# Raw-x products with two shift columns at three norms, and two-by-two wide tiles, in a two-layer encoder trunk

## The chip, the cores and the metric

The kernel runs on one core of one Trainium2 chip. The metric is the device time of one execution in microseconds (us); less is better. The engines are TensorE (PE in the profile; its weight loads are PEld), VectorE (DVE), ScalarE (ACT), GpSimd (POOL) and SyncE (SP), which issues the loads.

## The reference, cut

Sequence 256, model width D = 2048, two layers, all float32. Each sub-layer's norm is modulated by a shift, a scale and a gate that come from the conditioning vector c through a large matrix (adaLN: 12288 outputs a layer).

```
for l in range(2):
    sh_a, sc_a, g_a, sh_m, sc_m, g_m = split(silu(c) @ w_ada[l] + b_ada[l], 6)
    h = rmsnorm(x) * (1 + sc_a) + sh_a
    proj = h @ w_in[l]                 # differential q, k, v; latents cq, ckv; rope key
    out_a = diff_attention(...)        # 4 heads of two maps
    out_b = mla_attention(rmsnorm(cq, g) @ w_uq, rmsnorm(ckv, g) @ w_ukv, ...)
    x = x + g_a * (concat(out_a, out_b) @ w_o[l])
    h = rmsnorm(x) * (1 + sc_m) + sh_m
    x = x + g_m * (square(relu(h @ w_mlp_in[l])) @ w_mlp_out[l])   # 2048 -> 8192 -> 2048
return rmsnorm(x) * final_norm_g
```

Here rmsnorm(x) = x / rms, with rms the root of the mean square over the 2048 features of a token.

## The kernel before

**Layout.** x stays on the chip, features on partitions: 16 row blocks of 128 features by 256 tokens (`self.x[:, k]`). A product h @ w is made as output tiles of 128 features by 256 tokens, summed in PSUM over 16 row blocks k. There are eight PSUM banks of 512 columns (`bank`).

**Precision.** Trunk products run in the reduced-precision format fp32r with each factor split in a high and a low part. `mac` (L177 to L179) issues three matmuls for a step: hi·hi, hi·lo and lo·hi. In the names of the profile, `ps<-h,hi` at L177 is h's high part with the weight's, L178 h's low part, L179 the weight's low part.

**Weights.** `weights` brings a tile of 128x2048 (or 128x1536) floats through SP's queue into one of five shared buffers (`raw`), ScalarE writes its two halves' `hi` (L141), VectorE the `lo` (L142). Four `hi` and four `lo` buffers hold two tiles, so conversion runs at most two tiles ahead. The same five buffers take the adaLN tiles (`ada`, 1 MB each, 192 in all); VectorE multiplies and sums each with the conditioning vector (L292). `rate` (the RATE constants) says how many adaLN tiles are loaded for each weight tile; `ada_need` (L317) forces, in the order of the plan, all those that a use needs and that are not there yet.

**Three ways to make tiles.** `by_k` (L214) takes a weight tile by rows: for a row block, all its output tiles, in up to eight banks. It is used behind a norm, where row blocks of h become ready one by one. `pair` (L204) makes two output tiles in one bank with `mac`. `wide` (L188) makes one tile from a 512-column matmul (the weight's high part with h's high and low parts side by side, L197) and a 256-column one (its low part, L198), alternating; two banks' halves are then added (`joined`, L788). Layer 0's MLP uses `pair`, layer 1's `wide`.

**A norm.** Squares of x are summed on VectorE (`sumsq`). `rstd` (L475) sums over partitions with one-column matmuls (L483), takes root and reciprocal of two columns, builds a diagonal matrix (L492) and multiplies ones by it (L493), so that 1/rms stands on every partition for each token. `modulated` makes h for two row blocks (L503 to L505), and `norm_then_by_k` (L529) goes on with `by_k` over the first 12 output tiles: half of `w_a` or `w_m0`.

**A layer.** Norm, input projection, attention, output projection: four row groups in by_k form (`w_oa`) for tiles 0 to 3, then `pair` for the twelve others (`w_ob`), each followed by `update` (x plus gate times product, L786) and `sumsq`. Then the second norm with `w_m0`, and `mlp`: four blocks of 16 hidden tiles (`w_m1`, then `relu2`), each multiplied with its part of the second matrix token by token in 512 columns (`rows`, L753, tiles `py`), summed in `y`, and turned back (`turned`, L762, tiles `yt`). Layer 1 starts with a norm and `w_a` again.

**What sets the order.** A scheduler orders each engine's instructions by the program and by when it expects operands. Only inside `mlp` TensorE keeps the order of the program.

## Time and profile before

| | us |
|---|---|
| median of 3 runs | 2257.03 (2255.21 to 2258.25) |
| profiled execution | 2257.35 |
| its span in the profile | 2255.3 |
| TensorE busy | 2187.8 |
| VectorE busy | 1578.3 |
| ScalarE busy | 1112.4 |
| GpSimd busy | 1.9 |

The span runs from the first to the last instruction recorded; 2.05 us lie around it. Busy times are sums of records, in which matmuls that are pipelined overlap their neighbours, so how long a matmul occupies TensorE is read from the distance of two starts, or from a stage's length divided by its matmuls. In rows of groups the last part tells how long the engine had idled ahead of them, and what ended it; in rows of the timeline the same stands in brackets.

### The profile page before, as it was taken

What the parts mean: (1) busy time and instruction counts of PE and PEld (TensorE: products, weight loads), DVE (VectorE), ACT (ScalarE), POOL (GpSimd) and SP (SyncE); (2) the same over time, 40 slices, a digit from 0 to 9 for tenths busy, and PEclk for the clock granted to TensorE, in tenths of its full rate; (3) what the DMA queues carried; (4) which work ended last, traced back from release to release, by engine and by line L of the source; (5) the groups of instructions that cost most, each with busy time, mean ns of one, the idle gap of its engine ahead of it and who ended that gap; (6) DMA issues with size and microseconds to landing.
All of it is one profiled execution on the core that took longest, in us unless ns stands there. A gap on an engine that the chain in (4) does not pass through costs nothing.

```text
span 2255.3 us, 33208 instructions
## 1 busy us (share of the span) xinstructions
PE 2187.8 (97%) x13516; PEld 1972.3 (87%) x13516; DVE 1578.3 (70%) x2047; ACT 1112.4 (49%) x1608; POOL 1.9 (0%) x10
## 2 busy tenths in 40 slices
PE   3999999999999999999999999999999999999997
PEld 2899889998899899899879998999888888888886
DVE  7889878887777777777788776666545545555555
ACT  2655654355454355345444465544645534544543
POOL 0000000000000000000000000000000000000000
PEclk9999999999999999999989999999999999999998
DMA  9988678898888878888769756665555555555551
GB/s 371 355 313 318 256 277 318 307 339 324 317 317 299 326 296 313 329 302 307 292 235 346 277 225 224 243 229 167 205 198 190 188 188 188 187 195 196 187 187 56
DMA packets 85258, 585.52 MB, mean 260 GB/s; under 512 B 9457, under 2 KB 9841, under 8 KB 20593
## 3 DMA queue, kind: packets, MB, share of 16 engines
q1 hardware_dynamic: 85106, 583.42, 70.1%
q8 instruction: 105, 1.72, 0.3%
q14 instruction: 47, 0.39, 0.0%
HBM read 581.28 MB, written 2.10 MB: 259 GB/s over the span
## 4 chain that ended last, share of the span: by engine, by line
PE 92%; DVE 5%; DMA 1%; ACT 1%; issue 1%; SPq 0%; DVEq 0%; ACTq 0%
PE py L753 31%; PE ps L197 9%; PE ps L177 7%; PE ps L178 7%; PE ps L179 7%; PE pk L177 5%; PE pk L178 4%; PE pk L179 4%; PE ps L198 4%; DVE ada L292 2%; PE pk L234 1%; PE pv L250 1%; PE pv L248 1%; PE pv L249 1%; PE po L880 1%
## 5 line engine op out<-in xcount | busy, mean ns | idle before, releaser
L142 DVE TENSOR_TENSOR lo<-raw,hi 128x1024 fp32r<-128x1024 f32 (+1 forms) x728 | 861.2, 1186 | 587.4 <-ACT hi L141 586.1
L141 ACT ACTIVATE hi<-raw 128x1024 fp32r<-128x1024 f32 (+1 forms) x728 | 747.1, 1029 | 895.4 <-PE py L753 380.3
L753 PE MATMUL py<-hi,hid 128*128 128x512 f32 x2048 | 560.5, 390 | 0.0
L753 PEld LDWEIGHTS py<-hi,hid 128*128 128x128 f32 x2048 | 383.9, 188 | 79.4
L292 DVE SCALAR_TENSOR_TENSOR ada<-ada,cond 128x2048 f32<-128x2048 f32 x192 | 438.3, 2286 | 7.3 <-ACT cond L336 6.8
L753 PE MATMUL py<-lo,hid 128*128 128x512 f32 x1024 | 326.0, 389 | 0.0
L197 PE MATMUL ps<-h,hi 128*128 128x512 f32 x832 | 294.1, 399 | 0.0
L177 PE MATMUL ps<-h,hi 128*128 128x256 f32 x1024 | 291.4, 285 | 0.0
L179 PE MATMUL ps<-h,lo 128*128 128x256 f32 x1024 | 291.2, 284 | 0.0
L178 PE MATMUL ps<-h,hi 128*128 128x256 f32 x1024 | 290.8, 284 | 0.0
L198 PE MATMUL ps<-h,lo 128*128 128x256 f32 x832 | 234.0, 281 | 0.0
L753 PEld LDWEIGHTS py<-lo,hid 128*128 128x128 f32 x1024 | 192.3, 188 | 39.8
L177 PE MATMUL pk<-h,hi 128*128 128x256 f32 x752 | 214.5, 290 | 3.9 <-ACT h L504 3.9
L178 PE MATMUL pk<-h,hi 128*128 128x256 f32 x752 | 215.4, 287 | 1.1 <-DVE h L505 1.1
L179 PE MATMUL pk<-h,lo 128*128 128x256 f32 x752 | 215.0, 287 | 0.0
L177 PEld LDWEIGHTS ps<-h,hi 128*128 128x128 f32 x1024 | 196.5, 192 | 0.4
L178 PEld LDWEIGHTS ps<-h,hi 128*128 128x128 f32 x1024 | 196.6, 192 | 0.4
L179 PEld LDWEIGHTS ps<-h,lo 128*128 128x128 f32 x1024 | 196.6, 192 | 0.3
L197 PEld LDWEIGHTS ps<-h,hi 128*128 128x128 f32 x832 | 156.4, 188 | 38.8
L198 PEld LDWEIGHTS ps<-h,lo 128*128 128x128 f32 x832 | 157.4, 189 | 0.1
L177 PEld LDWEIGHTS pk<-h,hi 128*128 128x128 f32 x752 | 146.6, 198 | 6.2 <-ACT h L504 6.2
L178 PEld LDWEIGHTS pk<-h,hi 128*128 128x128 f32 x752 | 147.3, 196 | 1.5 <-DVE h L505 1.5
(209 smaller groups left out, 2568.6 us busy)
## 6 DMA issues: line engine op xcount, KB each, us to landing
raw<-in_w_m SPq DMA_DIRECT2D x232, 1024.0 KB, 4.9
ada<-in_w_ada SPq DMA_DIRECT2D x192, 1024.0 KB, 5.0
raw<-in_w_ob SPq DMA_DIRECT2D x24, 1024.0 KB, 5.0
raw<-in_w_m SPq DMA_DIRECT2D x32, 768.0 KB, 4.4
raw<-in_w_dv SPq DMA_DIRECT2D x16, 1024.0 KB, 4.8
raw<-in_w_a SPq DMA_DIRECT2D x20, 768.0 KB, 6.6
raw<-in_w_t SPq DMA_DIRECT2D x12, 1024.0 KB, 5.6
w<-in_w_a SPq DMA_DIRECT2D x24, 384.0 KB, 5.5
```

The source lines that it names most:

```text
L141: nc.scalar.activation(hi, v, AF.Copy)
L142: ins = nc.vector.tensor_tensor(lo, v, hi.bitcast(F32), ALU.subtract)
L177: mm(ps, hi, x[0], start=first, stop=False, skip_group_check=shared)
L178: mm(ps, hi, x[1], start=False, stop=False, skip_group_check=shared)
L179: mm(ps, lo, x[0], start=False, stop=last, skip_group_check=shared)
L197: mm(ps.rearrange("p a b -> p (a b)"), hi, both, start=k == 0, stop=False)
L198: mm(ps[:, 0], lo, x, start=False, stop=k == nk - 1)
L234: self.nc.tensor.matmul(ps, w[i][:, j * P : j * P + P], whole[i], start=first, stop=last, skip_group_check=True)
L248: mm(ps, xh, hi, start=first and k == 0, stop=False)
L249: mm(ps, xh, lo, start=False, stop=False)
L292: ins = nc.vector.scalar_tensor_tensor(w, w, 1.0, self.cond, ALU.mult, ALU.mult, accum_out=acc[:, i : i + 1])
L753: nc.tensor.matmul(out, stationary, v, start=start, stop=stop)
```

## The change

It does four things.

1. At three norms (layer 0's MLP, layer 1's attention, layer 1's MLP) the first six output tiles are multiplied with x·(1+scale) instead of h, as soon as a row block of x is complete (`ahead_part`). Two columns more hold the shift, twice the same, made by two small GpSimd operations for two row blocks, so a matmul has 258 columns. The six banks (`pa`) are multiplied with 1/rms and given the shift's product when they leave PSUM (`scaled`, `relu2` with a bias). `ahead_rest` puts the norm's sum over partitions behind step 1 of 8; from step 2 on, `modulated` makes h for everything else. The six other tiles of the by_k stage join the tiles behind it.
2. `rstd` sums with a matrix of 1/n, so that root and reciprocal work on 256 columns on all partitions; the diagonal is gone.
3. `wides` takes two tiles together, all 512-column matmuls of both ahead of all 256-column ones. It replaces `pair` in layer 0's MLP, `wide` in layer 1's, and by_k and `pair` for layer 1's differential q and k (`two`).
4. TensorE keeps the program's order from the `ob` pairs on, no more from the MLP on alone.

```diff
+TX = T + 2
+NAHEAD = 6
...
-    def wide(self, src, xs):
-
-        ps = self.bank("ps")
+    def wides(self, srcs, xs):
+
+        mm = self.nc.tensor.matmul
         nk = len(xs)
-        w = self.weights(src, nk * P)
         per = nk // 2
-        mm = self.nc.tensor.matmul
-        for k, (x, _, both) in enumerate(xs):
-            hi, lo = (v[:, (k % per) * P : (k % per) * P + P] for v in w[k // per])
-            mm(ps.rearrange("p a b -> p (a b)"), hi, both, start=k == 0, stop=False)
-            mm(ps[:, 0], lo, x, start=False, stop=k == nk - 1)
-        return ps
-
-    def wides(self, srcs, xs):
-        return [self.wide(src, xs) for src in srcs]
+        pss = [self.bank("ps") for _ in srcs]
+        ws = [self.weights(src, nk * P) for src in srcs]
+        part = lambda w, i, k: w[k // per][i][:, (k % per) * P : (k % per) * P + P]
+        for ps, w in zip(pss, ws):
+            for k, (_, _, both) in enumerate(xs):
+                mm(ps.rearrange("p a b -> p (a b)"), part(w, 0, k), both, start=k == 0, stop=False)
+        for ps, w in zip(pss, ws):
+            for k, (x, _, _) in enumerate(xs):
+                mm(ps[:, 0], part(w, 1, k), x, start=False, stop=k == nk - 1)
+        return pss
...
     def rstd(self, acc, n):
 
         nc = self.nc
-        ps = [self.bank("pn") for _ in range(2)]
-        r = self.s("rms")
+        ps = self.bank("pn")[:, 0]
         acc = acc[:2] + acc[3:]
         for i, a in enumerate(acc):
-            for t in range(2):
-                nc.tensor.matmul(
-                    ps[t][:, 0, :1], a[:, t * P : (t + 1) * P], self.ones[:, :1], start=i == 0, stop=i == len(acc) - 1
-                )
-        for t in range(2):
-            nc.scalar.activation(r[:, t : t + 1], ps[t][:, 0, :1], AF.Sqrt, bias=self.eps, scale=1.0 / n)
+            nc.tensor.matmul(ps, self.mean[n], a, start=i == 0, stop=i == len(acc) - 1)
+        r = self.cp.tile([P, T], F32, tag="rstd", name=self.name("rstd"), bufs=2)
+        nc.scalar.activation(r, ps, AF.Sqrt, bias=self.eps)
         nc.vector.reciprocal(r, r)
-        d = self.tp.tile([P, T], F32, tag="t", name=self.name("diag"))
-        for t in range(2):
-            c = slice(t * P, (t + 1) * P)
-            nc.vector.tensor_scalar(d[:, c], self.ident, r[:, t : t + 1], None, ALU.mult)
-        nc.tensor.matmul(ps[0][:, 1], self.ones, d, start=True, stop=True)
-        return ps[0][:, 1]
-
-    def modulated(self, r, k, sh, sc, whole):
+        return r
+
+    def ahead(self, l, sh, sc, src):
+
+        return SimpleNamespace(l=l, sh=sh, sc=sc, src=src, parts=[], banks=None, r=None)
+
+    def ahead_part(self, st, k):
+
+        nc = self.nc
+        for g in (st.sh, st.sc):
+            self.ada_need(st.l, g, k + 1)
+        sh, sc = self.mod[st.l, st.sh], self.mod[st.l, st.sc]
+        hi, lo = (self.flat(s, F32R).rearrange("p (a b) -> p a b", a=2) for s in ("ah", "al"))
+        both = sh[:, k : k + 2].unsqueeze(2).broadcast_to([P, 2, 2])
+        nc.gpsimd.tensor_copy(hi[:, :, T:], both)
+        nc.gpsimd.tensor_tensor(lo[:, :, T:], both, hi[:, :, T:].bitcast(F32), ALU.subtract)
+        for i in range(2):
+            x, c = self.x[:, k + i], sc[:, k + i : k + i + 1]
+            nc.scalar.activation(hi[:, i, :T], x, AF.Copy, scale=c)
+            nc.vector.scalar_tensor_tensor(lo[:, i, :T], x, c, hi[:, i, :T].bitcast(F32), ALU.mult, ALU.subtract)
+            st.parts.append((hi[:, i], lo[:, i]))
+
+    def ahead_step(self, st, p):
+
+        if st.banks is None:
+            st.banks = [self.bank("pa").rearrange("p a b -> p (a b)") for _ in range(NAHEAD)]
+        for i, w in enumerate(self.weights(st.src[p], 2 * NAHEAD * P)):
+            k = 2 * p + i
+            for j, ps in enumerate(st.banks):
+                self.mac(ps[:, :TX], w, j * P, P, st.parts[k], k == 0, k == NK - 1)
+
+    def ahead_rest(self, st, first, acc, after):
+
+        h = []
+        for p in range(first, 8):
+            if p == after:
+                r = self.rstd(acc, D)
+            self.ahead_step(st, p)
+            if p >= after:
+                upto = NK * (p - after + 1) // (8 - after)
+                while len(h) < upto:
+                    h += self.modulated(r, len(h), self.mod[st.l, st.sh], self.mod[st.l, st.sc])
+        st.r = r
+        return h
+
+    def scaled(self, st, b, out):
+
+        nc = self.nc
+        c = self.s("ac")
+        for i in range(2):
+            ps = st.banks[b + i]
+            nc.scalar.activation(c[:, i : i + 1], ps[:, T : T + 1], AF.Copy)
+            nc.vector.tensor_tensor(out[:, i], ps[:, :T], st.r, ALU.mult)
+        return out, c
+
+    def modulated(self, r, k, sh, sc, whole=None):
...
+            def two(i, dst, scale):
+                ps = self.wides([io["w_q"][0, i + j] for j in range(2)], h)
+                dst.append(self.joined(ps, self.u("qk"), scale))
+
+            two(0, q, qs)
+            two(8, kk, -1.0)
+            ckv += self.latent([ckr], gkv)
+            for hd in range(1, HD):
+                two(2 * hd, q, qs)
+                probs(hd - 1)()
+                two(8 + 2 * hd, kk, -1.0)
+                if hd == 1:
+                    cq += self.latent(cqr, gq)
+            keys()
...
-        for m in range(0, NK, 2):
-            if m < 4:
-                self.update(m, banks[m // 2], g)
-            else:
+        st = self.ahead(l, 3, 4, io["w_m0"][l])
+        for m in range(0, 4, 2):
+            self.update(m, banks[m // 2], g)
+            acc = self.sumsq(acc, self.x[:, m : m + 2])
+            self.ahead_part(st, m)
+        with self.tc.manual_schedule(engines={mybir.EngineType.PE}):
+            for m in range(4, NK, 2):
                 self.update(m, self.pair([io["w_ob"][l, m - 4 + j] for j in range(2)], o), g)
-            acc = self.sumsq(acc, self.x[:, m : m + 2], m == NK - 2)
-
-        self.rate = RATE_K
-        h, banks = self.norm_then_by_k(l, acc, 3, 4, io["w_m0"], 3, 0)
-        self.rate = RATE_M
-        g = self.mod[l, 5]
-        with self.tc.manual_schedule(engines={mybir.EngineType.PE}):
-            return self.mlp(l, h, banks, g)
-
...
+        nxt = None if l == DEPTH - 1 else self.ahead(l + 1, 0, 1, io["w_a1"][0])
         for fb in range(NFB):
             hid = []
-            for m in range(0 if fb else 12, NK, 2):
-                srcs = [io["w_m1"][l, NK * fb + m + j - 12] for j in range(2)]
-                ps = self.wides(srcs, h) if l else self.pair(srcs, h)
-                for b in banks:
-                    hid += self.relu2(b)
-                banks = []
-                hid += self.relu2(self.joined(ps, self.t("sum")) if l else ps)
+            for m in range(0 if fb else NAHEAD, NK, 2):
+                pss = self.wides([io["w_m1"][l, NK * fb + m + j - NAHEAD] for j in range(2)], h)
+                if m == NAHEAD and fb == 0:
+                    for b in range(0, NAHEAD, 2):
+                        hid += self.relu2(*self.scaled(st, b, self.t("sum")))
+                hid += self.relu2(self.joined(pss, self.t("sum")))
...
+                if cols == (3,) and nxt:
+                    self.ahead_step(nxt, 0)
...
+        acc = self.turned(3, y, g, acc, nxt, nxt is None)
+        if nxt:
+            self.rate = RATE_K
+            return self.ahead_rest(nxt, 1, acc, 2), nxt
+        return acc, None
...
         for m in range(4 * c, 4 * c + 4, 2):
...
             self.update(m, ps, g)
             acc = self.sumsq(acc, self.x[:, m : m + 2], last and m == NK - 2)
+            if nxt:
+                self.ahead_part(nxt, m)
```

In the diff's last hunks, the first two lines with `nxt` stand in the loop over `py` of layer 0's last block (`mlp`), the last ones in `turned`. Not shown: the weights are laid out anew (`w_m0` and `w_a1` hold six tiles, `w_q` layer 1's q and k, `w_m1` the rest), `joined` takes a scale, `stream` is written out in `rows`, the conditioning vector is scaled by 2048 against the 1/2048 in the new matrix.

**How instructions move.** The first place is SP's queue of loads at the end of layer 0's output projection (`raw<-in_w_ob` and `raw<-in_w_m` are weight tiles, `ada` adaLN tiles). Before:

```order
L153 DMA raw_3723<-in_w_ob 128x2048
L284 DMA ada_3735<-in_w_ada 128x2048
L153 DMA raw_3785<-in_w_ob 128x2048
L284 DMA ada_3796<-in_w_ada 128x2048
L153 DMA raw_3852<-in_w_ob 128x2048
L284 DMA ada_3864<-in_w_ada 128x2048
L153 DMA raw_3914<-in_w_ob 128x2048
L284 DMA ada_3925<-in_w_ada 128x2048
L153 DMA raw_4014<-in_w_m 128x1536
```

And now:

```order
L158 DMA raw_3824<-in_w_ob 128x2048
L289 DMA ada_3835<-in_w_ada 128x2048
L289 DMA ada_3892<-in_w_ada 128x2048
L289 DMA ada_3895<-in_w_ada 128x2048
L158 DMA raw_3908<-in_w_ob 128x2048
L289 DMA ada_3918<-in_w_ada 128x2048
L158 DMA raw_3968<-in_w_ob 128x2048
L289 DMA ada_3979<-in_w_ada 128x2048
L289 DMA ada_4036<-in_w_ada 128x2048
L289 DMA ada_4039<-in_w_ada 128x2048
L158 DMA raw_4057<-in_w_m 128x1536
```

The loads alternated one to one; now one or three adaLN tiles stand between two weight tiles. From the first `ob` tile to the first `w_m0` tile there are 21 adaLN loads, 13 before; in the eight `w_m0` tiles there are five.

The second place is VectorE's queue at the same point: the last `ob` tile's low halves (`lo`, 128x1024), the update of x from the last bank, and the first `w_m0` halves (128x768). Before:

```order
L142 TENSOR_TENSOR lo_3917<-raw_3914,hi_3916 128x1024
L142 TENSOR_TENSOR lo_3921<-raw_3914,hi_3920 128x1024
L292 SCALAR_TENSOR_TENSOR ada_3864,macc_82<-ada_3864,cond 128x2048
L142 TENSOR_TENSOR lo_4017<-raw_4014,hi_4016 128x768
L142 TENSOR_TENSOR lo_4021<-raw_4014,hi_4020 128x768
L786 SCALAR_TENSOR_TENSOR x<-ps_3851,mod_77,x 128x256 x2
```

And now (`al` is the low part of x·(1+scale), `acc` the sum of squares):

```order
L147 TENSOR_TENSOR lo_3975<-raw_3968,hi_3974 128x1024
L297 SCALAR_TENSOR_TENSOR ada_3918,macc_80<-ada_3918,cond 128x2048
L297 SCALAR_TENSOR_TENSOR ada_3979,macc_80<-ada_3979,cond 128x2048
L297 SCALAR_TENSOR_TENSOR ada_4036,macc_82<-ada_4036,cond 128x2048
L858 SCALAR_TENSOR_TENSOR x<-ps_3907,mod_77,x 128x256 x2
L313 TENSOR_TENSOR mod_79<-macc_80,vec 128x2
L297 SCALAR_TENSOR_TENSOR ada_4039,macc_82<-ada_4039,cond 128x2048
L478 TENSOR_TENSOR acc_3171<-acc_3171,sqx_4031 128x512
L311 SCALAR_TENSOR_TENSOR mod_81<-macc_82,vec 128x2
L147 TENSOR_TENSOR lo_4060<-raw_4057,hi_4059 128x768
L510 SCALAR_TENSOR_TENSOR al_4044<-x,mod_81,ah_4043 128x256 x2
L147 TENSOR_TENSOR lo_4064<-raw_4057,hi_4063 128x768
```

Between the last `ob` half and the first `w_m0` half stood one adaLN sum; now four stand there, with the last update of x and the accumulation.

The third place is TensorE at layer 0's MLP norm, from the last `ob` matmul on. Before:

```order
L179 MATMUL ps_3851<-do_3062,lo_3921 128x256
L483 MATMUL pn_3981<-ones,sqa_3977 128x1
L483 MATMUL pn_3982<-ones,sqa_3977 128x1
L483 MATMUL pn_3981<-ones,sqa_3979 128x1
L483 MATMUL pn_3982<-ones,sqa_3979 128x1
L493 MATMUL pn_3981<-diag_3995,ones 128x256
L177 MATMUL pk_3999<-h_4006,hi_4016 128x256
L177 MATMUL pk_4000<-h_4006,hi_4016 128x256
L177 MATMUL pk_4001<-h_4006,hi_4016 128x256
```

And now, at the start of the `pa` matmuls and, in the second fence, behind step 1, 72 of them later:

```order
L184 MATMUL ps_3907<-do_3037,lo_3975 128x256
L182 MATMUL pa_4051<-ah_3173,hi_4059 128x258
L183 MATMUL pa_4051<-al_3174,hi_4059 128x258
L184 MATMUL pa_4051<-ah_3173,lo_4060 128x258
L182 MATMUL pa_4052<-ah_3173,hi_4059 128x258
```

```order
L183 MATMUL pa_4056<-al_3187,hi_4111 128x258
L184 MATMUL pa_4056<-ah_3186,lo_4112 128x258
L487 MATMUL pn_4152<-acc_3171,mean_100 128x256 x2
L182 MATMUL pa_4051<-ah_3325,hi_4160 128x258
L183 MATMUL pa_4051<-al_3326,hi_4160 128x258
L184 MATMUL pa_4051<-ah_3325,lo_4161 128x258
```

The sum over partitions (`pn`) stood between the last product of the old stage and the first of the new; now it stands inside the new one, and the first `pa` matmuls need the `lo` half of the first `w_m0` tile.

165 lines of the change are left out of this document (93 added, 72 removed).

## The prediction

> **What bounds the kernel now.** I read the busy shares first, then the chain that ended last.
>
> ```profile
> PE 2187.8 (97%) x13516; PEld 1972.3 (87%) x13516; DVE 1578.3 (70%) x2047; ACT 1112.4 (49%) x1608; POOL 1.9 (0%) x10
> PE 92%; DVE 5%; DMA 1%; ACT 1%; issue 1%; SPq 0%; DVEq 0%; ACTq 0%
> ```
>
> TensorE sets the time. The span goes down only where it streams less or waits less, and up where something is late for it. Next the stages, as windows (columns: stretch, its length, busy time of PE, PEld, DVE, ACT, POOL, granted clock, DMA share, GB/s). In order they are: the start; layer 0's `ob` tiles; the gap of its MLP norm (A); that MLP's by_k stage; its `py` and pair stages; the gap ahead of layer 1 (B) and the by_k stage behind it; the gap of layer 1's MLP norm (C) and its by_k stage; layer 1's `wide` stage.
>
> ```profile
> 125.00:157.00 32.00, 30.43 (x244) 29.53 (x243) 29.84 (x38) 12.60 (x17) 0.00 (x0) 1.00 0.99 380
> 357.70:427.60 69.90, 69.90 (x586) 69.90 (x585) 62.79 (x74) 27.25 (x30) 0.00 (x0) 1.00 0.91 349
> 427.60:433.50 5.90, 2.19 (x14) 1.53 (x13) 5.39 (x12) 3.03 (x7) 0.00 (x0) 0.93 0.93 319
> 433.50:505.30 71.80, 71.52 (x575) 71.52 (x576) 62.29 (x85) 36.59 (x55) 0.00 (x0) 0.96 0.87 314
> 528.30:615.40 87.10, 87.10 (x388) 72.17 (x387) 62.96 (x61) 38.38 (x41) 0.00 (x0) 1.00 0.84 317
> 615.40:707.50 92.10, 92.10 (x768) 92.06 (x767) 68.09 (x74) 47.69 (x63) 0.00 (x0) 1.00 0.84 311
> 1156.00:1167.10 11.10, 6.20 (x27) 4.88 (x26) 7.70 (x16) 2.96 (x7) 0.00 (x0) 0.67 0.60 211
> 1167.10:1262.00 94.90, 94.68 (x767) 94.68 (x768) 77.12 (x100) 45.16 (x62) 0.00 (x0) 0.97 0.83 299
> 1515.40:1521.20 5.80, 3.41 (x22) 2.55 (x20) 3.25 (x9) 2.23 (x6) 0.00 (x0) 0.74 0.40 135
> 1521.20:1592.00 70.80, 70.52 (x575) 70.53 (x576) 42.05 (x64) 36.44 (x55) 0.00 (x0) 0.97 0.53 176
> 1701.70:1792.10 90.40, 90.40 (x513) 78.49 (x512) 48.96 (x62) 51.81 (x78) 0.00 (x0) 1.00 0.54 188
> ```
>
> Two things stand here. Layer 0 runs with VectorE at 90% in the `ob` stage and the DMA at 91%, where 99% was 380 GB/s: little is free there. Layer 1's MLP has room in both.
>
> **Streaming.** The pair stage is 768 matmuls of 256 columns in 92.1 us: 119.9 ns each. The `py` stage is 384 of 512 columns (four records are its neighbours') in 87.1 us: 226.8 ns. The `wide` stage is 256 pairs of one 512 and one 256 in 90.4 us: 353.1 ns a pair, more than 119.9 + 226.8 = 346.7. The new `wides` runs all 512 first, then all 256, so a k step of a tile pair's half costs 346.7 where three by three cost 359.7: 13.0 ns saved against pairs, 6.4 against the alternating form. An output pair has 32 such steps. Layer 0's MLP has 29 pairs (12.1 us), layer 1's q and k eight (3.3), its MLP 26 alternating ones (5.3) and three that were by_k (1.2): 21.9 us. The 864 matmuls of 258 columns: 256 and 512 lie 106.9 ns apart for 256 columns, so two columns are 0.8 ns, 0.7 us together (ends 0 and, if 258 were priced as 512, 92; it is nearest to 256). **−21.2 us.**
>
> The saving rests on 13 ns that every matmul costs beside its columns (119.9 − 106.9). The Trainium skill ("TensorE: Matmul & The Clock Gate", section Back-to-back issue gap) gives columns / 2.4 + 2.5 ns for matmuls without weight loads. By that fixed part the saving would be some 4 us (an estimate from the page). The two rows above, with a weight load for each matmul, disagree with it.
>
> **The three waits that go.** Gap A is 5.9 us, and its by_k stage 71.8 for 576 matmuls that stream in 69.1: 8.6 in all. B is 11.1 plus 94.9 − 92.1 (768 matmuls): 13.9. C is 5.8 plus 70.8 − 69.1: 7.5. Together 30.0. The work of TensorE that stays is the sum over partitions and B's transposes.
>
> ```profile
> 73.39 10.52 PE L234 MATMUL pk<-hf,w 128*128 128x256 f32 x48
> 1156.23 0.33 PE L769 MATMUL yt<-ident,y 128*128 128x128 f32 x1
> 1156.91 0.98 PE L769 MATMUL yt<-ident,y 128*128 128x128 f32 x7 [0.35 <-DVE y L729]
> ```
>
> A full-precision pass of 256 columns takes 219 ns here; the new `pn` is two matmuls of two passes, 0.9 us, three times. With B's eight transposes, 1.7 us from 1156.23 to 1157.89, 4.4 us stay. **−25.6 us.** The new chain from x to 1/rms (update, square, accumulation, `pn`) is hidden by the `pa` matmuls of steps 0 and 1, 8.7 us long (72 × 0.121), if those are fed; root and reciprocal lie beside step 2.
>
> **The wait that comes: A.** `ahead_part` needs shift and scale of each row block while the `ob` tiles still run. So adaLN loads that were spread by the rate are forced earlier: 21 of them now stand between the first `ob` tile and the first `w_m0` tile on SP's queue, 13 before, and their sums stand ahead of the weight halves in VectorE's queue.
>
> ```profile
> L142 DVE TENSOR_TENSOR lo<-raw,hi 128x1024 fp32r<-128x1024 f32 x624 | 762.1, 1224 | 539.6 <-ACT hi L141 538.7
> L142 DVE TENSOR_TENSOR lo<-raw,hi 128x768 fp32r<-128x768 f32 x104 | 99.1, 957 | 47.8 <-ACT hi L141 47.4
> L292 DVE SCALAR_TENSOR_TENSOR ada<-ada,cond 128x2048 f32<-128x2048 f32 x192 | 438.3, 2286 | 7.3 <-ACT cond L336 6.8 <-DMA ada<-in_w_ada 0.5
> L505 DVE SCALAR_TENSOR_TENSOR h<-ht,mod,h 128x256 fp32r<-128x256 f32 x64 | 28.5, 481 | 0.0
> L472 DVE TENSOR_TENSOR acc<-acc,sqx 128x512 f32<-128x512 f32 x33 | 22.7, 688 | 1.0 <-ACT sqx L471 0.4
> 351.34 1.22 DVE L142 TENSOR_TENSOR lo<-raw,hi 128x1024 fp32r<-128x1024 f32 x1
> 420.64 2.36 DVE L142 TENSOR_TENSOR lo<-raw,hi 128x1024 fp32r<-128x1024 f32 x2
> 428.11 0.88 DVE L786 SCALAR_TENSOR_TENSOR x<-ps,mod,x 128x256 f32<-128x256 f32 x2 [1.16 <-PE ps L179]
> ```
>
> Queued back to back, instructions overlap by some 85 ns (the two halves take 2.36, not 2 × 1.22), so I take 1.14, 0.87, 2.21, 0.395 and 0.605 us for these five. From the first `ob` half to the first `w_m0` half VectorE has 24 halves (27.4), 21 sums (46.4), ten small sums of modulation (0.8), 16 updates of x (6.3), seven accumulations (4.2), 14 new low parts (5.5) and the first 768 half (0.9): 91.5 us, and I add two waits of 1.16 for a finished bank, 93.8. TensorE streams those twelve tiles in 12 × 48 × 0.1199 = 69.1. VectorE starts 6.6 us ahead (351.34 against the stage at 357.9). So TensorE comes out 93.8 − 6.6 − 69.1 = 18.1 us late. The DMA agrees: 33 tiles of 1.049 MB are 34.6 MB, 91 us at 380 GB/s, on the edge; I add 1.2 us for that. In the `pa` stage VectorE has 16 halves, five sums and 32 steps of the modulation, 37 us with its rests, against TensorE's 34.8 (288 × 0.121), which leaves a tail I take as 1.9. **+21.2 us**; the ends are 0 (the scheduler's queue is not in the way) and 31 (the DMA at 349 GB/s, below).
>
> **B and C.** Ahead of layer 1 the adaLN loads aren't denser (rate K), but VectorE has 16 halves (13.9), five sums (11.1) and 32 modulation steps (12.6) and some 4.4 us of the last row blocks, 42 us against 34.8. The two tiles converted ahead in the `py` stage cover about five; **+2.2** (ends 0 and 7.2). At C no adaLN load is left and DVE is at 59% of the old stage: 0. The adaLN loads that were moved up at A are missing later, in layer 0's MLP, whose DVE had 24 us to spare in 92: it only gets lighter, worth nothing.
>
> **Small edits.** Nine norms lose the diagonal step, two records each, and with it a trip from VectorE to TensorE:
>
> ```profile
> L493 PE MATMUL pn<-diag,ones x18: 377/416/767, 29.1 to 2245.6; 128*128 128x256 f32 x18
> 420.56 0.16 DVE L308 TENSOR_TENSOR mod<-macc,vec 128x2 f32<-128x2 f32 x1
> L839 DVE RECIPROCAL r<-tot 128x2 f32<-128x2 f32 x32 | 5.2, 161 | 4.3 <-ACT sm L836 2.2 <-ACT s L836 2.0
> L793 DVE TENSOR_TENSOR sum<-ps,sum 128x256 f32<-128x256 f32 x52 | 21.7, 418 | 0.3 <-ACT sum L792 0.3
> ```
>
> In each of the four latent norms two passes of 0.22 go, −1.8 in all; at the end these and the trip, an estimate of −1. The RECIPROCAL grows from two to 256 columns. At two it costs 161 ns, as the TENSOR_TENSOR of two columns does, so I take that operation's 0.42 for 256; the ends are 0.16 and, since two columns hide a dearer one, 2 us. At A, B, C step 2 hides it; in the four latents and at the end it stands on the path, 0 to +8 us. Scaling on leaving PSUM (three times six matmul results, 0.42 each) and joining layer 0's and q's halves lie on VectorE beside 11.1 us of streaming a pair, of which it uses about nine (four halves 4.6, 1.3 sums 3.0, joining and splitting 1.3); that is the thinnest cover, worth +1 by my guess at lost waits (0 to 5).
>
> **Sum**, against the profiled execution: 2257.35 (span 2255.3 and 2.05 around it, 0.3 above the median 2257.03): −21.2 −25.6 +21.2 +2.2 −2.8 +1 = −25.2, so **2232 us**.
>
> **The rivals.**
>
> *VectorE's queue is not in the way at A* (the scheduler puts halves ahead of sums, or its lead is larger). For it: before, VectorE was 6.6 us ahead with 90% of the stage filled. Against: 91.5 us of work. Then 21.2 and 2.2 go: 2208. Chance 0.12.
>
> *The DMA, not VectorE, sets A.* 34.6 MB at the 349 GB/s of the old `ob` stage are 99 us, 8 more, and with the tail 2 more: 2242. Against it: that stage's DMA was not asked for more. 0.15.
>
> *Slower: the fast rows do not hold for 512-column streams into two banks in turn.* Other 512-column matmuls of the program show a longer record than `py`:
>
> ```profile
> L753 PE MATMUL py<-hi,hid 128*128 128x512 f32 x2048 | 560.5, 390 | 0.0
> L248 PE MATMUL pv<-hi,h 128*128 128x512 f32 x128 | 53.0, 414 | 0.0
> ```
>
> If `wides` ran like `pv`, 24 ns more on its 2112 wide matmuls are +51: 2283. It turns into a loss from 25.2 / 2112 = 12 ns on. Against it: the alternating form lies only 6.4 ns above the sum of its parts. 0.06.
>
> *GpSimd blocks VectorE.* The change puts 48 small operations there, 16 at each norm. The only price in the trace is a memset.
>
> ```profile
> L812 POOL MEMSET kr<- 128x512 f32 x2 | 1.1, 526 | 1143.2 <-PE yt L769 1032.3 <-PE pb L427 111.0
> ```
>
> If each held VectorE for that long at A, where its queue is the path, 16 × 0.526 = 8.4 us: 2240. No run before shows the two engines side by side. The Trainium skill ("SBUF — State Buffer", section Who interferes with whom) says that a VectorE operation with two SBUF inputs, which `lo` and `ada` are, and a GpSimd one that reads SBUF exclude each other for a whole instruction. 0.06.
>
> *The streaming saves nothing* (the fixed 13 ns belong to the weight load and stay with the columns): 2232 + 21 = 2253, within 0.2%. The rows speak against it. 0.03.
>
> **How the numbers follow.** The forecast has 0.58. Its own terms, one up and one down, give 2222 to 2241. The range goes down to the first rival and up past the second and the GpSimd case: 2208 to 2246; outside lie the two last dear cases and the edge, about 0.1 to 0.2. A measurement of this kernel tells some 0.2%, 4.5 us, from no change: faster is the forecast, the first, second and GpSimd cases but for their tails, 0.89; same 0.05; slower 0.06.
>
> **What would show it.** In the changed profile layer 0's `ob` stage lasts 88 us, not 69.9, with VectorE near full and TensorE waiting for `lo`; the three gaps shrink to a `pn` of 0.9 us inside `pa`; layer 0's MLP stages of four pairs take 88.8 us, not 92.1, and layer 1's 88.8, not 90.4. I am wrong if the `ob` stage keeps 70 us, if those stages keep 92.1, or if TensorE waits behind `scaled` or the 256-column reciprocal.

## The result, and the profile after

The changed kernel takes 2275.45 us (median of 4 runs, 2272.99 to 2276.42) against 2256.12 for the kernel before (4 runs): a ratio of 1.0083, with a 95% interval of 1.0065 to 1.0100. It is slower by some 19 us. The forecast was 2232, with a range up to 2246. One execution of a_half_load below took 2443.96 us at a granted clock of 0.84, and is left out of the figures of that kernel.

The first lines of the profile of the changed kernel (its profiled execution took 2272.99 us) are the busy times and the chain that ended last:

```profile
PE 2178.0 (96%) x12154; PEld 1889.0 (83%) x12154; DVE 1627.9 (72%) x2166; ACT 1159.2 (51%) x1731; POOL 38.5 (2%) x59
PE 89%; DVE 7%; DMA 1%; ACT 1%; issue 1%; DVEq 0%; ACTq 0%; SPq 0%
```

TensorE issues 1362 records fewer and is busy 10 us less, and VectorE's share of the chain went from 5% to 7%. So the change did its streaming work, and put waits in somewhere. The same stages as in the prediction, as windows of the changed kernel: layer 0's `ob` tiles; steps 0 and 1 of its `pa` stage; the other six steps; `py`; wide tiles; the `pa` stage ahead of layer 1 with the last transposes; the `pa` stage of layer 1's MLP; its wide tiles.

```profile
362.40:453.70 91.30, 74.60 (x580) 73.17 (x578) 86.33 (x109) 32.14 (x44) 9.70 (x9) 0.92 0.97 365
453.70:466.40 12.70, 10.87 (x71) 10.61 (x72) 9.98 (x14) 4.92 (x8) 1.58 (x2) 0.74 0.80 285
466.40:499.40 33.00, 27.53 (x222) 26.80 (x221) 31.06 (x53) 18.64 (x34) 0.00 (x0) 1.00 0.68 250
556.60:645.60 89.00, 89.00 (x387) 72.18 (x386) 65.31 (x66) 37.72 (x41) 0.00 (x0) 1.00 0.86 324
645.60:735.20 89.60, 89.60 (x512) 78.27 (x511) 67.95 (x85) 53.26 (x79) 0.00 (x0) 1.00 0.79 300
1184.30:1226.30 42.00, 39.30 (x300) 37.98 (x299) 40.11 (x66) 23.36 (x39) 0.00 (x0) 0.96 0.71 249
1534.00:1569.40 35.40, 35.40 (x294) 35.30 (x294) 31.02 (x54) 22.98 (x40) 0.00 (x0) 1.00 0.55 194
1714.50:1804.10 89.60, 89.60 (x513) 78.24 (x513) 46.05 (x60) 53.68 (x79) 0.00 (x0) 1.00 0.50 183
```

Three things are to be seen. The `ob` stage takes 91.3 us where its matmuls stream in 69.1, with VectorE at 95% and the DMA at 97%; the two `pa` windows take 45.7 instead of 34.8 + 0.9. At layer 1's MLP norm nothing waits: 35.4. And the `py` window, whose 384 matmuls the change did not touch, takes 89.0 us where it took 87.1, with TensorE busy all through at full clock: 231.8 ns a matmul, not 226.8.

From the starts of the stages' first matmuls in the two traces (us) comes where the time went; the forecast column splits the sum of the prediction over the same stretches (without its +1 for lost waits and the 0.7 for 258 columns).

| stretch | before | after | difference | forecast |
|---|---|---|---|---|
| start to layer 0's `ob` tiles | 357.7 | 362.4 | +4.7 | −0.9 |
| `ob` tiles to the first `py` (A) | 170.6 | 194.2 | +23.6 | +12.3 |
| rest of layer 0's MLP | 627.7 | 627.7 | 0.0 | −10.8 |
| layer 1 up to its `ob` tiles (B) | 290.3 | 281.8 | −8.5 | −13.3 |
| `ob` tiles to the first `py` (C) | 168.3 | 159.2 | −9.1 | −7.8 |
| rest of layer 1's MLP | 622.6 | 628.3 | +5.7 | −5.3 |
| end | 18.1 | 17.6 | −0.5 | −1.0 |

The two MLPs miss their gain by 22 us in all, A by 11, the start and B by 5 each.

### The profile page after: what moved, and what is told of

Read it like the earlier page. It is cut to its first block, busy times and chain, and to the rows that moved or that the text cites. A ratio compares the mean times of both kernels' runs of the same rounds, so it can differ in the third digit from the quotient of the medians.

```text
span 2271.2 us, 30768 instructions
## 1 busy us (share of the span) xinstructions
PE 2178.0 (96%) x12154; PEld 1889.0 (83%) x12154; DVE 1627.9 (72%) x2166; ACT 1159.2 (51%) x1731; POOL 38.5 (2%) x59
## 4 chain that ended last, share of the span: by engine, by line
PE 89%; DVE 7%; DMA 1%; ACT 1%; issue 1%; DVEq 0%; ACTq 0%; SPq 0%
PE ps L203 21%; PE ps L206 11%; PE py L828 10%; PE py L826 10%; PE py L830 10%; DVE ada L297 3%; PE pk L239 3%; PE ps L184 2%; PE ps L183 2%; PE ps L182 2%; DVE lo L147 1%; PE pv L255 1%; PE pv L253 1%; PE pv L254 1%; PE pa L184 1%; PE pa L183 1%
## 5 line engine op out<-in xcount | busy, mean ns | idle before, releaser
L203 PE MATMUL ps<-h,hi 128*128 128x512 f32 x2112 | 503.4, 395 | 0.9 <-ACT hi L146 0.9
L203 PEld LDWEIGHTS ps<-h,hi 128*128 128x128 f32 x2112 | 392.5, 188 | 89.1 <-ACT hi L146 1.4
L297 DVE SCALAR_TENSOR_TENSOR ada<-ada,cond 128x2048 f32<-128x2048 f32 x192 | 437.7, 2286 | 7.4 <-ACT cond L343 6.9
L826 PE MATMUL py<-hi,hid 128*128 128x512 f32 x1024 | 331.3, 394 | 0.0
L830 PE MATMUL py<-hi,hid 128*128 128x512 f32 x1024 | 330.8, 394 | 0.0
L206 PEld LDWEIGHTS ps<-h,lo 128*128 128x128 f32 x2112 | 259.2, 188 | 5.9
L206 PE MATMUL ps<-h,lo 128*128 128x256 f32 x2112 | 260.8, 281 | 0.0
L184 PE MATMUL pa<-ah,lo 128*128 128x258 f32 x288 | 83.9, 291 | 9.3 <-DVE lo L147 9.3
L239 PE MATMUL pk<-hf,w 128*128 128x256 f32 x288 | 65.4, 388 | 22.6 <-DMA w<-in_w_a 22.6
L182 PE MATMUL pa<-ah,hi 128*128 128x258 f32 x288 | 83.8, 291 | 2.5 <-ACT hi L146 2.5
L183 PE MATMUL pa<-al,hi 128*128 128x258 f32 x288 | 83.1, 288 | 0.0
L239 PEld LDWEIGHTS pk<-hf,w 128*128 128x128 f32 x288 | 56.1, 195 | 31.4 <-ACT h L554 23.3
L184 PE MATMUL ps<-moh,lo 128*128 128x256 f32 x192 | 56.6, 295 | 9.3 <-DVE lo L147 9.3
```

The source lines that it names most:

```text
L182: mm(ps, hi, x[0], start=first, stop=False, skip_group_check=shared)
L183: mm(ps, hi, x[1], start=False, stop=False, skip_group_check=shared)
L184: mm(ps, lo, x[0], start=False, stop=last, skip_group_check=shared)
L203: mm(ps.rearrange("p a b -> p (a b)"), part(w, 0, k), both, start=k == 0, stop=False)
L206: mm(ps[:, 0], part(w, 1, k), x, start=False, stop=k == nk - 1)
L239: self.nc.tensor.matmul(ps, w[i][:, j * P : j * P + P], whole[i], start=first, stop=last, skip_group_check=True)
```

## The experiments

My theory after the result was in two parts. First, that the matmuls' durations changed because the 258-column tiles gave all 40 shared activation buffers another pitch (2080 bytes a partition, not 2048), so that operands begin at other addresses. Second, that A waits because loads and VectorE's sums are both full there.

### The pitch alone: b_pad32 and b_pad64

```diff
 # the kernel before
+TX = T + 2                      # b_pad64: T + 8
...
+    def flat(self, name, dt=F32):
+        return self.up.tile([P, 2 * TX], dt, tag="u", name=self.name(name))
     def u(self, name, dt=F32):
-        return self.up.tile([P, 2, T], dt, tag="u", name=self.name(name))
+        return self.flat(name, dt)[:, : 2 * T].rearrange("p (a b) -> p a b", a=2)
...
```

Of b_pad32 was expected: 

> The kernel before, with nothing changed but the pitch of its 40 shared activation buffers (h, hid, y, the attention's tiles): 2080 bytes a partition, as the change has it for its two shift columns, where it was 2048. Theory (addresses): the 512-column py matmuls, whose start distance went from 226.8 to 232.1 ns with the change though their instructions are the same, go to about 232 here as well (3072 of them, +16 us), the 256-column ones from 120.0 to about 118.3 as in the changed kernel (some 8200, -13 us), and the whole ends within 2252 to 2268 us against 2256. Rival (not the addresses but the order of the matmuls around, or traffic of other engines): py stays at 226.8, the 256-column ones at 120.0, and the time is that of before within 0.2%.

Measured: 2257.0 us against 2255.79, ratio 1.0005 (0.9996 to 1.0014). The windows of layer 0's first `py` stage, of its pair stage behind it and of layer 1's first wide stage:

```profile
525.20:614.50 89.30, 89.30 (x388) 72.20 (x386) 63.09 (x61) 38.53 (x41) 0.00 (x0) 1.00 0.85 317
614.50:705.30 90.80, 90.80 (x769) 90.75 (x768) 67.93 (x74) 47.65 (x63) 0.00 (x0) 1.00 0.84 314
1700.20:1789.60 89.40, 89.40 (x513) 78.06 (x512) 48.95 (x61) 51.89 (x78) 0.00 (x0) 1.00 0.54 189
```

The instructions are those of the kernel before, and `py` takes 89.3 us (87.1), the pairs 90.8 (92.1), the alternating tiles 89.4 (90.4). So the pitch does it: a 512-column matmul of `py` takes 232.0 ns from its start to the next one's (226.8 before), a 256-column one of the pairs 118.2 (90.8 / 768; 119.9 before). For the kernel before, with its 8176 narrow and 4400 wide matmuls, the two nearly cancel. For the changed kernel, which turns narrow ones into wide ones, they don't.

Of b_pad64 was expected: 

> As b_pad32, with a pitch of 2112 bytes, so that every buffer begins at a multiple of 64 bytes. In the changed kernel py took 233.2 ns where the stationary operand began 32 bytes beyond a multiple of 64, and 230.8 elsewhere. If only that offset of 32 costs, py is 227 here; if the addresses matter up to 256 or 512 bytes, py is 229 to 231 (+7 to +13 us from py). If addresses don't matter at all: 226.8.

Measured: 2255.65 us, ratio 1.0000 (0.9990 to 1.0009); `py` is 230.6 ns on average, as in the middle case. Sorting the 3072 `py` matmuls by where their stationary operand (a 128-column slice of `hid`, 512 bytes a partition) begins, from the buffers' addresses in the built program, gives this:

```
kernel    start of the stationary operand, bytes    mean start to start, ns (matmuls)
before    0 mod 512                                 226.8 (3066)
b_pad64   0 / 64 / 128 / 192 mod 256                228.2 (1056) / 233.2 (768) / 232.7 (479) / 229.9 (763)
b_pad32   0 / 32 mod 64                             230.8 (1535) / 233.1 (1531)
```

The moving operand of `py` is a weight tile, which begins at a multiple of 512 bytes in all three. So the place of the stationary operand alone moves a 512-column matmul by some 6 ns. What in the chip makes it so isn't shown.

### The tiles two by two alone: b_wides

```diff
 # the kernel before, with wides of the change
-                ps = self.wides(srcs, h) if l else self.pair(srcs, h)
+                ps = self.wides(srcs, h)
...
-                hid += self.relu2(self.joined(ps, self.t("sum")) if l else ps)
+                hid += self.relu2(self.joined(ps, self.t("sum")))
```

Expected: 

> The kernel before with one part of the change alone: its MLPs' tiles two by two, all 512-column matmuls ahead of the 256-column ones, on the old pitch of 2048 bytes; norms as before. If the terms of my sum hold on the old addresses (226.8 + 119.9 = 346.7 a step against 359.7 and 353.1), 26 pairs of layer 0 save 10.8 us and 26 of layer 1 save 5.3: 2240 us. Rival 1 (512- and 256-column matmuls cost 235 and 117 with h as moving operand whatever the order, as in layer 1 before): 5.5 us saved in layer 0, 2250.5. Rival 2 (joining the banks makes VectorE or ScalarE late in layer 0): above 2256.

Measured: 2240.86 us, ratio 0.9935 (0.9921 to 0.9950): 15 us faster than before, 16.1 expected. It beats both kernels. The windows of `py`, of layer 0's wide stage and of layer 1's:

```profile
527.70:614.80 87.10, 87.10 (x388) 72.15 (x387) 64.58 (x64) 37.92 (x41) 0.00 (x0) 1.00 0.86 328
614.80:703.70 88.90, 88.90 (x513) 78.71 (x512) 68.91 (x86) 53.33 (x79) 0.00 (x0) 1.00 0.82 314
1690.00:1778.90 88.90, 88.90 (x513) 78.71 (x512) 46.10 (x61) 53.83 (x79) 0.00 (x0) 1.00 0.51 185
```

Both wide stages take 88.9 us for 256 steps, 347.3 ns each, nearly the 346.7 of 226.8 + 119.9; neither VectorE nor ScalarE is late. The first rival of this run, that h as moving operand costs more in any order, falls; it was the alternation that cost 6 ns.

### The shift's columns taken out of the change: a_no_shift

The shift is left out of the first six tiles here, with GpSimd's work for it.

```diff
 # the changed kernel
-TX = T + 2
+TX = T
...
-        nc.gpsimd.tensor_copy(hi[:, :, T:], both)
-        nc.gpsimd.tensor_tensor(lo[:, :, T:], both, hi[:, :, T:].bitcast(F32), ALU.subtract)
...
-            nc.scalar.activation(c[:, i : i + 1], ps[:, T : T + 1], AF.Copy)
+            nc.scalar.activation(c[:, i : i + 1], ps[:, T - 1 : T], AF.Copy)
```

Expected: 

> The changed kernel with the two shift columns left out (so is the shift's product; the bias is taken from a token's column to keep the instruction), pitch of the activation buffers back at 2048 bytes, no work on GpSimd. Theory (addresses): py returns to 227 ns and the wides to 227 + 120, which over 3072 py, 2112 wide and 2112 narrow matmuls is 15.7 + 12 - 3 = 25 us, less 1.4 ns on some 4700 256-column ones, 7: about 2257; the waits of layer 0 stay. Rival (GpSimd's work and its lock on VectorE's port cost): the matmuls stay at 232, and only the ob and pa waits fall, by up to 8 us.

Measured: 2254.99 us, ratio to before 0.9996 (0.9987 to 1.0006), so 20.5 less than the changed kernel. The windows of `ob`, of the whole `pa` stage, of `py` and of the wide tiles:

```profile
367.00:458.10 91.10, 75.33 (x580) 73.69 (x578) 86.27 (x109) 32.05 (x44) 0.00 (x0) 0.92 0.95 365
458.10:503.80 45.70, 38.37 (x291) 37.37 (x292) 41.12 (x67) 23.57 (x42) 0.00 (x0) 0.93 0.73 258
560.70:647.80 87.10, 87.10 (x388) 72.15 (x387) 65.23 (x65) 37.73 (x41) 0.00 (x0) 1.00 0.88 331
647.80:736.70 88.90, 88.90 (x513) 78.70 (x512) 68.10 (x85) 53.36 (x79) 0.00 (x0) 1.00 0.79 302
```

`py` and the wides are back at 87.1 and 88.9, while `ob` and `pa` wait as long as with GpSimd's work (91.1 and 45.7, against 91.3 and 45.7). Over 3072 matmuls of `py` (eight such stages) and 2112 wide steps this is 15.2 and 5.8 us; the narrow matmuls that are left go the other way, as in b_pad32. So the 20 us are put down to the pitch (the two profiled executions lie 16.1 apart), and GpSimd costs nothing in `ob` and `pa`. The changed kernel shows why, in GpSimd's and VectorE's timelines:

```profile
400.10 0.19 POOL L505 CAST ah<-mod 128x4 fp32r<-128x4 f32 x1 [13.25 <-DVE mod L313]
433.65 2.12 POOL L505 CAST ah<-mod 128x4 fp32r<-128x4 f32 x1 [15.45 <-DVE mod L313]
```

```profile
399.88 0.87 DVE L858 SCALAR_TENSOR_TENSOR x<-ps,mod,x 128x256 f32<-128x256 f32 x2
433.43 2.29 DVE L297 SCALAR_TENSOR_TENSOR ada<-ada,cond 128x2048 f32<-128x2048 f32 x1
```

The same cast of four columns takes 0.19 us beside an update of x, which reads one of its two tiles from PSUM, and 2.12 beside an adaLN sum, which reads two from SBUF: it ends when the sum does. The sums are not longer for it: 2286 ns on average in both kernels.

### Layer 0's norm as before: a_no_a

```diff
 # the changed kernel, layer 0's MLP norm only
+            r = self.rstd(acc, D)
+            banks = self.open_banks(3)
+            for p in range(8):
...
+                h += self.modulated(r, k, self.mod[l, 3], self.mod[l, 4])
+                self.by_k(banks, [io["w_m0"][l, p]], h, k, NK, 6)
```

Expected: 

> The changed kernel without its first part at layer 0's MLP norm: there the twelve ob tiles, the norm and a by_k stage of six tiles with h stand as before, adaLN loads are not forced early and GpSimd has nothing to do there; the two later norms and the wides stay. Theory (VectorE's queue full of adaLN sums at that place): the 32 us that TensorE waited in the ob and pa stages go, 9 to 12 us of gap and by_k wait come back: 2250 to 2256 us. Rival (VectorE's work is only put off, its debt comes due in the by_k and wides stages of layer 0): 2265 to 2275.

Measured: 2261.17 us, ratio to before 1.0026 (1.0015 to 1.0038). That is 14 us better than the changed kernel where I expected 19 to 25, and not what the rival said. The `ob` stage, the gap, and the by_k stage of six tiles:

```profile
362.60:435.30 72.70, 68.86 (x580) 68.45 (x579) 66.38 (x79) 29.24 (x33) 0.00 (x0) 0.99 0.94 352
435.30:442.10 6.80, 2.07 (x4) 1.17 (x4) 6.76 (x10) 0.75 (x2) 0.00 (x0) 0.50 0.95 360
442.10:486.20 44.10, 39.17 (x287) 38.67 (x288) 42.38 (x64) 19.50 (x32) 0.00 (x0) 0.86 0.76 299
```

The `ob` stage is short again, so it is what the change adds to that stage, the early adaLN work and the parts of x·(1+scale), that stretches it. But a by_k stage of six tiles streams in some 34 us (288 × 0.119), and VectorE is busy for 42.4 of its 44.1 us, with h and the weights' low halves: as I read it, half a stage no longer covers that work.

### Loads or sums: a_half_sum, a_half_load, a_half_both

In these half of each adaLN sum is left out, or half of each load (the half that comes is then summed twice, in two instructions), or both.

```diff
 # the changed kernel; a_half_both has both edits
-        self.nc.sync.dma_start(w, self.io["w_ada"][l, NK * g + i])
+        self.nc.sync.dma_start(w[:, : D // 2], self.io["w_ada"][l, NK * g + i][:, : D // 2])
...
-                w, w, 1.0, self.cond, ALU.mult, ALU.mult, accum_out=acc[:, i : i + 1]
+                w[:, : D // 2], w[:, : D // 2], 1.0, self.cond[:, : D // 2], ALU.mult, ALU.mult, accum_out=acc[:, i : i + 1]
```

Of a_half_sum was expected: 

> The changed kernel with each adaLN sum on VectorE over half of its columns (1024 of 2048; half of the conditioning product is left out), the loads as they are. Theory (VectorE's queue sets layer 0's ob and pa stages): 21 sums there are some 23 us shorter, so the 32 us that TensorE waits in these two stages fall to under 12, and the stage ahead of layer 1 gains some 4: 2275 goes to about 2248. Rival (the loads set them: 33 MB-tiles between the first ob and the first w_m0 tile take 91 us at 380 GB/s whatever VectorE does): at least 20 us of the waits stay, ScalarE waits for the raw tiles, and the time is above 2262.

Of a_half_load: 

> The counterpart: each adaLN tile brings only half of its columns, and VectorE sums that half twice, so its work is as long as before (two instructions of some 1.2 us for one of 2.29). Theory (VectorE): the waits in layer 0's ob and pa stages stay within 26 to 34 us, the time at 2268 to 2276. Rival (loads): they fall to under 12 us, and the time to about 2250.

Of a_half_both: 

> The changed kernel with half of each adaLN tile loaded and half of it summed (half of the conditioning product left out). With the sums alone halved TensorE still waited 25.9 us in layer 0's ob stage (loads at 353 GB/s), with the loads alone halved 18.1. Theory (both the loads and VectorE's queue are full there, either alone holds the stage at 87 to 95 us): with both halved the ob stage takes 68 to 72 us, and the waits of ob and pa together are under 8. Rival (a third thing holds it, the order of the queue or ScalarE): ob stays above 80.

Measured: 2251.91, 2261.16 and 2223.33 us (ratios to before 0.9985, 0.9976 to 0.9994; 1.0022, 1.0012 to 1.0031; 0.9853, 0.9838 to 0.9868). The `ob` window and the `pa` window of each; first with the sums halved:

```profile
349.20:444.20 95.00, 76.59 (x580) 74.89 (x578) 67.43 (x113) 32.88 (x46) 7.33 (x10) 0.89 0.91 353
444.20:485.40 41.20, 38.53 (x290) 37.75 (x291) 34.33 (x61) 21.82 (x39) 0.00 (x0) 0.92 0.76 277
```

with the loads halved:

```profile
354.10:441.30 87.20, 73.03 (x578) 71.84 (x577) 83.69 (x143) 32.26 (x44) 7.08 (x10) 0.92 0.71 248
441.30:487.60 46.30, 39.58 (x295) 38.65 (x294) 45.24 (x80) 23.91 (x41) 1.00 (x1) 0.93 0.70 238
```

with both:

```profile
340.00:415.10 75.10, 70.45 (x579) 69.84 (x578) 64.26 (x109) 32.00 (x44) 7.33 (x10) 0.98 0.80 285
415.10:453.30 38.20, 36.44 (x295) 35.65 (x294) 36.76 (x66) 23.63 (x39) 0.00 (x0) 1.00 0.80 276
```

With VectorE's sums halved it is idle 29% of the `ob` stage, and the stage still lasts 95.0 us. I took that for the loads: the DMA moves 353 GB/s there, and 33 tiles (34.6 MB) at that rate are 98 us, a few of them brought ahead. But the waits in that stage of a_half_sum name something else:

```profile
ACT sqx L477 <- DVE x L858: 44.5, 4, 13.2
PE ps L182 <- ACT hi L146: 12.7, 3, 4.7
ACT hi L146 <- DMA raw<-in_w_ob: 3.8, 2, 2.3
```

ScalarE waits for weight tiles for 3.8 us only (24.8 in the changed kernel, below). It stands 8 to 13 us at a time at `sqx`, the squares of an x that TensorE has not finished, and the next tile's `hi` is behind that in its queue: the tile issued at 410.9 us had landed at 416.6 in the trace, and its `hi` began at 424.9. So a_half_sum does not show what the loads alone would do; the order of ScalarE's queue came between. In a_half_both the wait for `sqx` is 0.7 us.

With the loads halved the DMA is at 71% and VectorE at 96%, and the stage lasts 87.2; both stages together are 28.7 us longer than they stream (69.1 + 35.7), within the 26 to 34 expected, and the time is 7 us below the expected range, as `ob` begins 8 us earlier. With both halved the stage lasts 75.1 us, somewhat above the 68 to 72 that I had expected, and that excess of both stages falls from 32 to 8.5 (75.1 + 38.2 − 69.1 − 35.7, against 91.3 + 45.7 less the same). So VectorE's sums hold the `ob` stage even with half the loads; with half the sums the loads, or the queue order that the scheduler chose with them, still hold it, and which of these two it is stays open. The `pa` stage follows the sums (41.2 with half of them, 46.3 with half the loads). For a_half_sum both the theory and the rival were wrong: the excess stayed (31.4 us), but not because ScalarE waited for loads, and the total came near the theory's (2251.9, 2248 expected) because attention ran ahead by 13 us as well (`ob` begins at 349.2, not 362.4).

### The sums spread over attention: a_rate16

```diff
 # the changed kernel
-RATE_A0, RATE_A1, RATE_A2, RATE_K, RATE_M = 1.1, 0.5, 0.7, 0.6, 0.66
+RATE_A0, RATE_A1, RATE_A2, RATE_K, RATE_M = 1.6, 0.5, 0.7, 0.6, 0.66
...
         st = self.ahead(l, 3, 4, io["w_m0"][l])
+        self.rate = 0.0
```

Expected: 

> The changed kernel with two numbers of the adaLN plan changed: rate A0 1.6 instead of 1.1 through layer 0's attention, and none but forced loads from the ob pairs on. On SP's queue 72 adaLN loads then stand ahead of the first ob tile (59 before) and 8 in the ob stage (21). VectorE was busy 73% in the attention's last 125 us, so 13 sums (29 us) fit there. Theory (the lag comes from the sums being crowded into the ob stage): the ob stage falls from 91 to 70-74 us, and the time to 2250-2258. Rival (VectorE's work up to that norm is too much wherever it stands): attention becomes later by as much, and the time stays above 2268.

Measured: 2262.74 us, ratio to before 1.0032 (1.0021 to 1.0043), between the two cases. The last part of attention, `ob`, and `pa`:

```profile
240.00:371.70 131.70, 126.80 (x724) 110.17 (x723) 111.83 (x164) 74.44 (x147) 6.70 (x12) 0.99 0.86 324
371.70:445.20 73.50, 70.23 (x578) 69.79 (x577) 66.07 (x85) 36.13 (x48) 7.52 (x4) 0.98 0.82 303
445.20:482.60 37.40, 36.41 (x295) 35.60 (x294) 36.90 (x59) 21.80 (x36) 0.00 (x0) 1.00 0.79 290
```

The `ob` stage falls to 73.5 us and `pa` to 37.4, as the theory said: 26 us fewer. But `ob` begins at 371.7 instead of 362.4: attention paid back nine of them, though VectorE had idle time there; what was late in it isn't shown.

### One step further: b_wides_qk

```diff
 # b_wides, with joined and two as in the change
-            col(i, dst, scale)()
+            two(i, dst, scale)
...
             probs(n)()
-            col(i + 1, dst, scale)()
```

Expected: 

> b_wides, and the six last q and k tiles of each layer's input projection two by two as well (old pitch, norms as before): six pairs of 32 steps at 13.0 ns save 2.5 us on b_wides' 2240.9: 2238.4. Rival (the pair now ends one tile later, so the attention scores queued between its tiles start later): no gain, 2240 to 2243.

Measured: 2246.17 us, 5.3 more than b_wides (ratios to before 0.9957, 0.9944 to 0.9969, against 0.9935). The rival's time was nearer, though it did not expect a loss of that size, and its wait was another one: the scores wait less than in b_wides (`psc`, 3.2 us there, none here), but TensorE now stands ahead of `pqr`, in the latent attention, for ScalarE's `qr`, here in layer 0:

```profile
PE pqr L828 <- ACT qr L267: 5.3, 1, 5.3
```

In layer 1 it is 3.2 us more; b_wides has neither wait. b_wides stays the best version.

## Why the prediction was wrong, point by point

**Streaming (−21.2 forecast): the step that failed.** "a k step of a tile pair's half costs 346.7 where three by three cost 359.7" is right on the buffers for which it was measured; b_wides shows 347.3. I carried both durations over to buffers that the change itself moves. On the new pitch the step costs 350.0 (89.6 us / 256, in both layers) against 355 for three narrow ones (3 × 118.2), so it saves 5 ns there and not 13, and `py`, of which the prediction says nothing, pays 5 ns on 3072 matmuls, 16 us. a_no_shift measures the whole at 20.5 us. The signs that I had named came out nearly as written (`ob` 91.3 us for 88, the wide stages 89.6 for 88.8); none of them looked at `py`. The group lines of `py` show it even where a window isn't drawn:

```profile
L826 PE MATMUL py<-hi,hid 128*128 128x512 f32 x1024 | 331.3, 394 | 0.0
```

394 ns, where the kernel before had 390 for the same line. The rival "512-column streams cost more" was thought of for the wides alone; the bound for 258 columns looked at their length and not at the buffer they need.

**The wait at A (+21.2 forecast): right mechanism, too small.** The `ob` stage lasts 22.2 us longer than it streams and `pa` 10.0 (91.3 − 69.1 and 45.7 − 35.7), 32 in all, and the five tile pairs behind them take 57.2 us where 160 steps of 350.0 ns are 56.0. For `ob` I had 18.1 + 1.2, for `pa` a tail of 1.9, so `pa` is the larger miss. In `ob` TensorE stands still for 16.7 us (91.3 − 74.6); most of the rest is its clock, which I had not priced. In two stretches of the changed kernel's `ob` stage half the clock was granted, and 256-column matmuls followed one another at 213 ns:

```profile
402.30:409.10 6.80, 4.27 (x20) 4.28 (x21) 6.80 (x11) 2.81 (x4) 0.00 (x0) 0.50 1.00 384
436.40:443.20 6.80, 5.60 (x26) 5.61 (x27) 6.53 (x8) 2.92 (x4) 0.00 (x0) 0.50 0.99 411
```

The first begins inside a stand of 4.4 us. So a stand here costs more than its own length: the stage's matmuls are busy 74.6 us, where the old stage's were 69.9.

The part that I added for the DMA should have been a bound of its own: at the 365 GB/s that it reached, not 380, 34.6 MB are 95 us. The rival "the DMA sets A" had that; since a_half_sum does not isolate the loads, no run shows it, and a_half_load shows that they alone aren't it. The waits of the changed kernel between 362 and 500 us name what was left out in `pa`:

```profile
ACT hi L146 <- DMA raw<-in_w_ob: 24.8, 6, 9.8
PE ps L184 <- DVE lo L147: 9.3, 4, 4.4
PE pa L184 <- DVE lo L147: 7.0, 4, 2.7
PE ps L182 <- ACT hi L146: 5.2, 2, 3.4
ACT rstd L489 <- PE pn L487: 4.4, 1, 4.4
DVE rstd L490 <- ACT rstd L489: 3.9, 1, 3.9
```

VectorE, the engine that is late, stands still for 3.9 us because the reciprocal is in its queue ahead of the weights' low halves and waits for a `pn` that TensorE reaches late; ScalarE stands 4.4 us at the root, with `hi` behind it. I had written that root and reciprocal "lie beside step 2"; on TensorE they do, on these two engines they block the queue.

**The reciprocal (0.42 us taken, 2 as the upper end).** It takes 1.75:

```profile
L490 DVE RECIPROCAL rstd<-rstd 128x256 f32<-128x256 f32 x9 | 15.7, 1750 | 8.3 <-ACT rstd L489 8.3
```

At the start and in two latents ahead of layer 0's `ob` tiles that is 1.3 us more each than I took, 4 in all, and that stretch lost 4.7 where −0.9 was forecast; but the traces don't put its loss there. At the start, TensorE's first products with h wait for a load, before and now:

```profile
47.03 12.27 PE L234 MATMUL pk<-hf,w 128*128 128x256 f32 x48 [16.75 <-DMA w<-in_w_a]
49.83 10.35 PE L239 MATMUL pk<-hf,w 128*128 128x256 f32 x37 [22.59 <-DMA w<-in_w_a]
```

That is 2.8 us, with 1/rms there at 30.9 us (30.7 before). The reciprocals of the two latents begin 1.6 and 1.2 us later than before, so the first of them delayed nothing up to the second. In attention TensorE waits 2.9 us longer for `psc` (6.1, 3.2 before) and 2.3 for `pqr` (none before). No run took the reciprocals away.

**B (+2.2 forecast for the tail)** is 5.7 (42.0 − 36.3: 288 matmuls of `pa`, `pn` and the eight transposes), within the bounds of 0 and 7.2 that I gave it. TensorE stands 2.7 us there (42.0 − 39.3), 2.3 of them for `lo`, and the clock is 0.96; that h and the low halves compete on VectorE, as at A, is argued.

**C** was right: nothing waits, 9.1 us gained with 7.8 forecast. It is the only norm at which no adaLN load is left and VectorE has room.

**GpSimd as a rival** was wrong in its direction. The Trainium skill ("SBUF — State Buffer", section Who interferes with whom) says of such a pair that the one which starts second waits; the two timelines above agree, with GpSimd as the one that waits, and nobody waits for GpSimd.

What stays open: what made the start 5 us worse than forecast in full, whether the loads alone can hold the `ob` stage, and why the place of an operand changes a matmul's duration.

## What to carry to other kernels

A duration read from a trace belongs to the buffers of that trace: where a change gives a pool another tile size, every matmul that reads from the pool may change by a few per cent, also those whose code is untouched, so keep the old pitch or price the new one first with a kernel that changes nothing else. Where two resources are both above 90% in a stage (here VectorE and the loads, joined by five buffers), work that is pulled ahead into it is paid for, and freeing one of them (half the sums, half the loads) left the stage at 95 and 87 us; look then at what the freed engine waits for, which may be the order of another engine's queue. Try the parts of a change one by one: one of the four parts here, and that only in the two MLPs, was worth 15 us by itself.

## What the runs showed of the hardware that I had not expected

- With buffers at a pitch of 2080 bytes, 512-column matmuls went from 226.8 to 232.0 ns, and 256-column ones from 119.9 to 118.2, in a program of the same instructions. The best case is a stationary operand that begins at a multiple of 256 bytes (228.2 on the pitch of 2112, 226.8 on 2048); the worst ones begin at an odd multiple of 32 (233.1), or 64 or 128 behind a multiple of 256 (233.2 and 232.7).
- Alternating 512- and 256-column matmuls cost 353.1 ns a pair, the same ones sorted by width 347.3.
- A GpSimd cast of four columns took 0.19 us beside a VectorE operation with one input in PSUM, and 2.12 beside one with two inputs in SBUF, which itself kept its 2.29.
- When TensorE had stood for some microseconds in the `ob` stage, half the clock was granted for 6.8 us (0.50 in two windows above), and 256-column matmuls took 213 ns from start to start.
- VectorE's RECIPROCAL costs 161 ns for two columns and 1750 for 256: 6.3 ns a column, where a TENSOR_TENSOR of 256 took 418 in all.
